# Expert gates in float32: one matmul per token in place of three, with the tokens innermost in the eviction

## The chip, the cores and the metric

The kernel runs on one core of a Trainium2 chip. The metric is the device time of one execution in microseconds, as the median of several runs. The profile is one execution, recorded by the hardware profiler.

## The reference, cut to what is computed

Two transformer blocks in float32 over 256 tokens of width 1024. The first ends in product-key experts, and only these are touched. Each token has 8 heads, each head picks 16 of 128 x 128 experts by two lists of sub-keys, and the gates are a softmax over the 16 scores:

```python
v1, i1 = lax.top_k(s1, PEER_TOPK)
v2, i2 = lax.top_k(s2, PEER_TOPK)
...
top_s, pos = lax.top_k(cand_s, PEER_TOPK)
idx = jnp.take_along_axis(cand_i, pos, axis=-1)
g = jax.nn.softmax(top_s, axis=-1)
u_sel = jnp.take(u_tab, idx, axis=0)
h = jnp.einsum('bthkd,btd->bthk', u_sel, xb)
a = (jax.nn.gelu(h.astype(jnp.float32)) * g).astype(xb.dtype)
return jnp.einsum('bthk,bthkd->btd', a, jnp.take(v_tab, idx, axis=0))
```

An expert's index is `i1 * 128 + i2`. A token thus has 128 picks (8 heads of 16), each with a pair of indices and a gate.

## The kernel before, in words

Nothing is gathered: the kernel multiplies all tokens with all 16,384 rows of the table u, and sets the unpicked experts to nought by a dense matrix of gates. The table comes in 128 chunks of 128 experts (512 KB each, loaded on the queue of SyncE into `rawt`, five ahead). A chunk is split into two parts of 12 significant bits (`wrt` by ScalarE, line 241; `wlt` by VectorE, line 242), and `mm_stat` (lines 447 to 451) multiplies it with the tokens in 24 matmuls of 256 columns. ScalarE evicts through gelu: the first 56 chunks (`NB`) go into `H`, which holds [128 experts, 56 chunks, 256 tokens], the others through `hs` to DRAM (`hsp`), except the last two pairs, which stay. Then `peer_v` reads the table v against the gated values.

Beside the chunks two generators run on VectorE, stepped by counted microseconds (`STEP`: 1.55 a chunk for `select`, 1.7 for `gates`; a step yields what it is reckoned to take). `select` finds the picks: the two top-16 lists, the candidates, the 16 best and their index pairs, and writes them transposed into `picks`, one column per token: row 0 the first index, row 1 the second, row 2 the gate, rows 3 and 4 what bfloat16 leaves of it. When it ends, `gates` starts, one group of four tokens for each chunk of u, 64 groups in all.

A group is one call of `prep` and one of `put`. `prep` compares the second and the first index of the 128 picks with the numbers 0 to 127, which gives one-hot rows [128 picks, 128, 4 tokens] in bfloat16, with the four tokens innermost, and multiplies the first of these with the three parts of the gate. `put` makes, for each token, three matmuls over the 128 picks into one [128, 128] block of gates; VectorE multiplies the first 56 columns of four tokens into `H` (line 848), and ScalarE copies the other 72 into `G` (line 849). `prep` runs one group ahead of `put`, with two buffers for its tiles.

The order of the instructions on each engine is set by a scheduler with a simulated timeline. Those that are pinned (`pin`) keep their place in the program: the first compare of a group, the gate matmuls, and the first matmul of each chunk in this stage. The others may be moved by the scheduler.

Of the kernel before, what the change touches and what calls it, by code (L numbers as in the profile page):

```python
# [8 lines left out]
F32 = mybir.dt.float32  # L9
# [16 lines left out]
WARM = (2.5, 0.5, 2, 1.5)  # keep_warm at the start, after the first transposes, before a block, in the mixer  # L26
STEP = (1.55, 1.7)  # steps of the selection and of the gates per chunk of peer_u
NB = 56  # expert blocks whose activations stay in SBUF
V_AFTER_R = (0, 0, 0, 0, 2, 2, 2, 2)  # chunks of w_v after each chunk of w_r
# [14 lines left out]
def _consts():  # L44
    """Constants of the shapes alone: [128, n] float32 blocks."""
    f = np.float32
    c = {}
    i = np.arange(128)
    c["ident"] = np.eye(128, dtype=f)
    c["iota"] = np.tile(i.astype(f)[None], (128, 1))  # L50
    half = 32
    freqs = (f(10000.0) ** (-np.arange(half, dtype=f) / f(half))).astype(f)
    ang = (np.arange(256, dtype=f)[:, None] * freqs[None]).astype(f)
    cs = np.stack([np.cos(ang), np.sin(ang)], 1).astype(f)
    c["rope"] = cs.reshape(2, 128, 2, 32).transpose(1, 0, 2, 3).reshape(128, 128)
    log_g = np.log1p(-np.exp2(-5.0 - np.arange(8, dtype=np.float64)))
    diff = (i[None, :] - i[:, None]).astype(np.float64)
    dm = np.zeros((128, 8, 256))
    for h in range(8):
        diag = np.where(diff >= 0, np.exp(log_g[h] * np.maximum(diff, 0)), 0)  # L60
        dm[:, h, :128] = diag
        dm[:, h, 128:256] = np.exp(log_g[h] * (diff + 128))
    c["dmask"] = dm.reshape(128, 8 * 256).astype(f)
    c["sblt"] = (i[:, None] < i[None, :]).astype(f)
    c["nsuf"] = -(i[:, None] >= i[None, :]).astype(f)
    p, q = i[:, None], i[None, :]
    same = (p // 64) == (q // 64)
    lt, le = (p < q) & same, (p <= q) & same
    dec = f(-math.exp(-0.5))
    c["tri"] = np.concatenate([le * dec, lt * dec], 1).astype(f)  # L70
    c["m4"] = np.concatenate([lt, lt, le, le], 1).astype(f)
    c["off"] = (same & (p // 16 > q // 16)).astype(f)
    q32 = np.arange(32)[None, :]
    c["m16"] = ((p // 16 % 2 == q32 // 16) & (p % 16 > q32 % 16)).astype(f)
    c["dl"] = (p % 16 == np.arange(16)[None, :]).astype(f)
    c["b8"] = (p // 16 == np.arange(8)[None, :]).astype(f)
    c["blk"] = same.astype(f)
    c["hs2"] = (i[:, None] // 64 == np.arange(2)[None, :]).astype(f)
    return c
# [29 lines left out]
def layout(inp):  # L109
    """Host side: the inputs in the layouts in which the kernel loads them."""  # L110
# [51 lines left out]
class Kern:  # L162
# [37 lines left out]
    def keep_warm(self, us, acc=False):  # L200
        """Matmuls into a bank that nobody reads, so that a wait doesn't halve TensorE's clock."""
# [18 lines left out]
    def add_mixed(self, names, order):  # L220
        """Chunks of several weights in turns: names[j] for each j of order."""
        at = [0] * len(names)
        for j in order:
            self.plan.append((names[j], self.d[names[j]][at[j]]))
            at[j] += 1
# [32 lines left out]
    def after(self, a, b):  # L258
        """a is issued after b, on the same engine."""
        self.tc.add_manual_dep(a.ins, b.ins.name, mybir.DependencyInfo(  # L260
            mybir.DependencyClass.NoSync, mybir.DependencyReason.DATA), reason="order")
# [12 lines left out]
    def steps(self, gens):  # L274
        """Each generator starts one step after the one before it."""
# [12 lines left out]
    def rsqrt(self, x, n, name="rs_y"):  # L288
        """x ** -0.5 on [128, n]."""
# [4 lines left out]
    def split(self, ps, r, l, scale=None, pin=False):  # L294
        """r + l = ps (times scale per partition), both with 12 significant bits."""
# [11 lines left out]
    def transposed(self, pool, src, nk, name, scale=None, plain=False, then=None, pin=False):  # L307
        """src(h, k): token-major [128, 128] blocks -> parts of the transpose, [128, nk, 256]."""
# [28 lines left out]
    def square(self, h, c0, c1, pin=False):  # L337
        """Sum of squares of some columns of the residual; after the last, the inverse norm."""
# [19 lines left out]
    def norm_T(self, pool, name, gname, g0, npool=None, nkw={}, plain=False, then=None):  # L358
        """rms-normalized residual, transposed, in parts."""
# [12 lines left out]
    def turn(self, k):  # L372
        """Two [128, 128] blocks of columns of the residual, transposed, in PSUM."""
# [9 lines left out]
    def res_T(self, pool, gain, pin=False):  # L383
        """The residual times the gain, transposed, in parts; its consumer scales the tokens by the inverse norm."""
# [12 lines left out]
    def uncap(self, n=1 << 30):  # L397
        """Splits of up to n more chunks of weights, in this place of the program."""
# [4 lines left out]
    def mm_mov(self, name, xr, xl, nk, evac, side=1, tail=0, pin=False, halves=True, marks={}):  # L403
        """One group of 512 columns: evac(h, psum) for the token halves h of x @ w.
        The first half is done earlier by the last `tail` chunks of weights."""
        nc = self.nc
        # token half, columns, psum
# [33 lines left out]
    def mm_stat(self, name, xr, xl, out, nk=8, pin=False):  # L441
        """out [128 features, 256 tokens] of the next chunk of weights."""
# [11 lines left out]
    def attn(self):  # L454
        nc, tc, d = self.nc, self.tc, self.d
        with ExitStack() as cx:
# [42 lines left out]
            def qk_norm(accs, idx, scale):  # L499
                """Heads of 64, rms-normalized: [128, 2, 512] token-major, gain not yet applied."""  # L500
# [120 lines left out]
            def pin(a):  # L621
                """Keeps the functions that need tables in their order, so that the tables change seldom."""
# [107 lines left out]
    def peer(self):  # L730
        nc, tc, d = self.nc, self.tc, self.d
        with ExitStack() as cx:
# [3 lines left out]
            with ExitStack() as cu:  # L736
                pu = cu.enter_context(tc.tile_pool(name="pu", bufs=1, reuse_waits="tile"))
                hw = cu.enter_context(tc.tile_pool(name="hw", bufs=2, reuse_waits="tile"))
                picks = pu.tile([128, 5, 256], BF, name="picks")
                H = pu.tile([128, NB, 256], F32, name="H")  # L740
                iota4 = pu.tile([128, 128, 4], BF, name="iota4")
                nc.vector.tensor_copy(iota4, self.iota[:, :, None].to_broadcast([128, 128, 4]))
# [25 lines left out]
                def select():  # L768
                    """Yields about the microseconds of VectorE that each step takes."""
# [5 lines left out]
                    for t in range(2):  # L775
# [44 lines left out]
                        nc.scalar.copy(picks[:, 0:3, tt], pt)  # L820
                        low = tk.tile([128, 128], F32, name="low")
                        nc.vector.tensor_tensor(low, pt[:, 2], picks[:, 2, tt], op=OP.subtract)
                        nc.scalar.copy(picks[:, 3, tt], low)
                        nc.vector.tensor_tensor(picks[:, 4, tt], low, picks[:, 3, tt], op=OP.subtract)
                        yield 1.3

                def gates(G):
                    """Per token: one-hot rows of the picks times the gates in three exact parts."""
                    def prep(t0):
                        ts = slice(t0, t0 + 4)  # L830
                        pk = [picks[:, None, j, ts].to_broadcast([128, 128, 4]) for j in range(5)]
                        oa = hw.tile([128, 2, 128, 4], BF, name="oa", tag="ar")
                        ob = hw.tile([128, 2, 128, 4], BF, name="ob", tag="al")
                        o = [oa[:, 0], oa[:, 1], ob[:, 0], ob[:, 1], oa[:, 0]]
                        pin(nc.vector.tensor_tensor(o[0], iota4, pk[0], op=OP.is_equal))
                        nc.vector.tensor_tensor(o[1], iota4, pk[1], op=OP.is_equal)
                        for j in range(2, 5):
                            nc.vector.tensor_tensor(o[j], o[0], pk[j], op=OP.mult)
                        return t0, o

                    def put(t0, o):
                        pg = self.sm.tile([128, 4, 128], F32, name="smt")
                        for t in range(4):
                            for j in range(2, 5):
                                pin(nc.tensor.matmul(pg[:, t], o[1][:, :, t], o[j][:, :, t],  # L845
                                                     start=(j == 2), stop=(j == 4)))
                        hv = H[:, :, t0:t0 + 4].rearrange("p i t -> p t i")
                        nc.vector.tensor_tensor(hv, pg[:, :, :NB], hv, op=OP.mult)  # L848
                        nc.scalar.copy(G[:, :, t0:t0 + 4].rearrange("p i t -> p t i"), pg[:, :, NB:])

                    old = prep(0)
                    yield 3
                    for t0 in range(4, 260, 4):
                        new = prep(t0) if t0 < 256 else None
                        put(*old)
                        old = new
                        yield 1.7
# [97 lines left out]
    def top16(self, pool, jobs, n):  # L955
        """The 16 largest of each x [128, n], largest first, and where they first stand: (val, idx, x)."""
# [121 lines left out]
    def rwkv(self):  # L1078
        nc, tc, d = self.nc, self.tc, self.d
        with ExitStack() as cx:  # L1080
# [36 lines left out]
            with ExitStack() as c1:  # L1117
# [17 lines left out]
                def chain(pt, k):  # L1135
                    """Parts of the mix for K, straight from the transposes, before what the others need."""
# [106 lines left out]
            with ExitStack() as c2:  # L1243
# [23 lines left out]
                def values():  # L1267
                    """Steps of one chunk of weights: 256 features of x @ w_v, token-major."""
# [16 lines left out]
                def prep(i, wk, M32):  # L1285
                    """Decayed A, B, K, R of two heads, in the places of their sources; M = A B^T."""
# [42 lines left out]
                def subst(i0, i1, wk, M32, sel):  # L1329
                    """Transposed inverses of the unit lower triangular 16 x 16 blocks, a row at a time."""  # L1330
# [302 lines left out]
```

## Time and profile before

| what | value |
|---|---|
| median of 3 runs | 1861.52 us (1861.39 to 1861.53) |
| span of the profiled execution, first to last instruction | 1859.7 us |
| PE (TensorE matmul) busy | 1844.6 us, 99% |
| DVE (VectorE) busy | 1348.8 us, 73% |
| ACT (ScalarE) busy | 990.7 us, 53% |
| gate matmuls, line 845 | 768 records, 483.7 to 755.8 us |

The profile gives no time for its execution other than the span; the runs' median is 1.8 us longer. The busy time of an engine is the union of its instructions. Matmuls are pipelined, so a record is longer than the time for which it holds the engine; the distance from one start to the next tells what it costs. PEld are the weight loads of TensorE, which run beside its matmuls.

### The profile page before, as it was taken

To read this page: it belongs to the slowest core of one execution; us is meant where nothing else is said; L and a number is where in the kernel's file an instruction comes from. 1 tells how busy PE (TensorE), PEld (TensorE's weight loads), DVE (VectorE), ACT (ScalarE), POOL (GpSimd) and SP (SyncE) were. 2 spreads that over 40 slices of the span, in tenths; PEclk is the share of its full clock that TensorE was granted. 3 is DMA by queue.
4 is the path that set the end of the run, shared out by engine and by line. 5 is a ranking of instruction groups with operands and counts; after the bars stand their busy time and mean duration, and the time that the engine had idled before them with its cause. 6 is when DMAs were issued, how large, how long until landed. Compare 5 with 4: busy or idle time off the path is not lost.

```text
span 1859.7 us, 31176 instructions
## 1 busy us (share of the span) xinstructions
PE 1844.6 (99%) x12249; PEld 1662.3 (89%) x12249; DVE 1348.8 (73%) x2532; ACT 990.7 (53%) x1557; POOL 63.6 (3%) x60
## 2 busy tenths in 40 slices
PE   9999999999999999999999999999999999999998
PEld 7877899999999999888888888899887988879997
DVE  6755668899888888655666667688657886558874
ACT  6468554445544444544444455566456744456653
POOL 1110000000000000000000000000002011000000
PEclk9999999999999999999999999999999999999999
DMA  7454545555644445556777755555653320035553
GB/s 276 138 169 147 173 149 169 182 182 181 187 150 158 154 154 156 186 192 196 221 269 240 242 193 181 158 184 182 229 173 97 117 67 1 1 103 190 185 186 121
DMA packets 90450, 308.59 MB, mean 166 GB/s; under 512 B 9981, under 2 KB 11517, under 8 KB 89918
## 3 DMA queue, kind: packets, MB, share of 16 engines
q1 hardware_dynamic: 90014, 306.07, 50.8%
q8 instruction: 96, 1.57, 0.3%
q10 hardware_dynamic: 288, 0.52, 0.1%
q14 instruction: 52, 0.43, 0.1%
HBM read 296.59 MB, written 9.96 MB: 165 GB/s over the span
## 4 chain that ended last, share of the span: by engine, by line
PE 97%; DVE 2%; DMA 1%; ACT 0%; issue 0%; SPq 0%; POOL 0%; POOLq 0%; ACTq 0%
PE acct L451 13%; PE acct L447 13%; PE acct L450 13%; PE acct L420 7%; PE acct L421 7%; PE acct L415 6%; PE acct L929 6%; PE acct L933 6%; PE acct L932 6%; PE smt L845 5%; PE acct L1423 1%; PE acct L1209 1%; PE smt L1394 1%; DVE wlt L242 0%; PE acct L1278 0%; PE acct L1279 0%
## 5 line engine op out<-in xcount | busy, mean ns | idle before, releaser
L242 DVE TENSOR_TENSOR wlt<-rawt,wrt 128x1024 fp32r<-128x1024 f32 x532 | 650.9, 1225 | 280.3 <-ACT wrt L241 278.9
L241 ACT CAST wrt<-rawt 128x1024 fp32r<-128x1024 f32 x532 | 556.1, 1046 | 296.8 <-PE acct L421 106.6
L447 PE MATMUL acct<-XR,wrt 128*128 128x256 f32 x1920 | 549.0, 287 | 0.0
L451 PE MATMUL acct<-XL,wrt 128*128 128x256 f32 x1920 | 542.7, 283 | 1.0 <-DVE XL L302 1.0
L450 PE MATMUL acct<-XR,wlt 128*128 128x256 f32 x1920 | 543.5, 283 | 0.0
L447 PEld LDWEIGHTS acct<-XR,wrt 128*128 128x128 f32 x1920 | 368.3, 192 | 1.6 <-issue 0.9
L451 PEld LDWEIGHTS acct<-XL,wrt 128*128 128x128 f32 x1920 | 367.3, 192 | 2.2 <-DVE XL L302 2.2
L450 PEld LDWEIGHTS acct<-XR,wlt 128*128 128x128 f32 x1920 | 368.0, 192 | 0.5 <-issue 0.2
L932 PE MATMUL acct<-wlt,ar 128*128 128x512 f32 x512 | 182.1, 389 | 0.0
L933 PE MATMUL acct<-wrt,al 128*128 128x512 f32 x512 | 181.6, 389 | 0.0
L929 PE MATMUL acct<-wrt,ar 128*128 128x512 f32 x512 | 138.9, 389 | 0.0
L420 PE MATMUL acct<-wlt,XR 128*128 128x512 f32 (+1 forms) x304 | 118.5, 391 | 0.5 <-DVE wlt L242 0.5
L421 PE MATMUL acct<-wrt,XL 128*128 128x512 f32 (+1 forms) x304 | 116.7, 392 | 0.0
L933 PEld LDWEIGHTS acct<-wrt,al 128*128 128x128 f32 x512 | 96.1, 188 | 20.0
L932 PEld LDWEIGHTS acct<-wlt,ar 128*128 128x128 f32 x512 | 96.1, 188 | 19.9
L929 PEld LDWEIGHTS acct<-wrt,ar 128*128 128x128 f32 x512 | 96.1, 188 | 19.9
L415 PE MATMUL acct<-wrt,XR 128*128 128x512 f32 (+1 forms) x304 | 112.1, 394 | 0.5 <-ACT wrt L241 0.5
L1069 ACT ACTIVATE z<-acct,cols 128x256 f32<-128x256 f32 x88 | 49.8, 566 | 90.9 <-PE acct L451 90.9
L845 PE MATMUL smt<-ob,oa 128*128 128x128 bf16 x512 | 93.9, 296 | 0.0
L845 PEld LDWEIGHTS <-oa 128*128 128x128 bf16 x768 | 81.7, 118 | 3.8
L877 ACT ACTIVATE hs<-acct 128x256 f32<-128x256 f32 x72 | 27.9, 387 | 105.7 <-PE acct L451 105.7
L848 DVE TENSOR_TENSOR H<-smt,H 128x224 f32<-128x224 f32 x64 | 42.9, 670 | 46.1 <-PE smt L845 46.1
(422 smaller groups left out, 2827.4 us busy)
## 6 DMA issues: line engine op xcount, KB each, us to landing
rawt<-in_peer_u SPq DMA_DIRECT2D x128, 512.0 KB, 3.5
rawt<-in_peer_v SPq DMA_DIRECT2D x128, 512.0 KB, 3.5
rawt<-in_ffn_up SPq DMA_DIRECT2D x88, 512.0 KB, 3.5
rawt<-in_w_in SPq DMA_DIRECT2D x52, 512.0 KB, 4.2
rawt<-in_ffn_dn SPq DMA_DIRECT2D x44, 512.0 KB, 3.4
hsp<-hs SPq DMA_DIRECT2D x34, 256.0 KB, 3.9
hs<-hsp SPq DMA_DIRECT2D x34, 256.0 KB, 3.6
rawt<-in_peer_wq SPq DMA_DIRECT2D x16, 512.0 KB, 3.6
```

The costliest lines, as they stand in the source:

```text
L241: c = nc.scalar.copy(r, t)
L242: v = nc.vector.tensor_tensor(l, t, r.bitcast(F32), op=OP.subtract)
L415: m = nc.tensor.matmul(o, a, wr, start=(k == 0), stop=False)
L420: nc.tensor.matmul(o, a, wl, start=False, stop=False)
L421: nc.tensor.matmul(o, b, wr, start=False, stop=(k == nk - 1))
L447: m = nc.tensor.matmul(out, wr, xr[:, k], start=(k == 0), stop=False)
L450: nc.tensor.matmul(out, wl, xr[:, k], start=False, stop=False)
L451: nc.tensor.matmul(out, wr, xl[:, k], start=False, stop=(k == nk - 1))
L845: pin(nc.tensor.matmul(pg[:, t], o[1][:, :, t], o[j][:, :, t], start=(j == 2), stop=(j == 4)))
L929: m = nc.tensor.matmul(acc[t][c], a, wr, start=first, stop=False)
L932: nc.tensor.matmul(acc[t][c], a, wl, start=False, stop=False)
L933: nc.tensor.matmul(acc[t][c], b, wr, start=False, stop=last)
```

## The change

The picks are kept in float32 (three rows instead of five), and the copy of the numbers 0 to 127, repeated for four tokens, goes. `prep` makes two float32 tiles [128 picks, 4 tokens, 128], with the 128 numbers innermost: the one-hot rows of the second index, and those of the first index times the gate. That is two compares and one product where two compares and three products were. `put` makes one float32 matmul per token. The eviction reads the block of gates with the tokens innermost, so `H` and `G` are touched in runs of four tokens, and PSUM with a stride of 128 elements. Comments go, and a constant `TG` of 4 comes; the groups and their steps stay.

```diff
+TG = 4
...
-                picks = pu.tile([128, 5, 256], BF, name="picks")
+                picks = pu.tile([128, 3, 256], F32, name="picks")
                 H = pu.tile([128, NB, 256], F32, name="H")
-                iota4 = pu.tile([128, 128, 4], BF, name="iota4")
-                nc.vector.tensor_copy(iota4, self.iota[:, :, None].to_broadcast([128, 128, 4]))
...
-                        nc.scalar.copy(picks[:, 0:3, tt], pt)
-                        low = tk.tile([128, 128], F32, name="low")
-                        nc.vector.tensor_tensor(low, pt[:, 2], picks[:, 2, tt], op=OP.subtract)
-                        nc.scalar.copy(picks[:, 3, tt], low)
-                        nc.vector.tensor_tensor(picks[:, 4, tt], low, picks[:, 3, tt], op=OP.subtract)
-                        yield 1.3
+                        nc.scalar.copy(picks[:, :, tt], pt)
+                        yield 0.8
...
                     def prep(t0):
-                        ts = slice(t0, t0 + 4)
-                        pk = [picks[:, None, j, ts].to_broadcast([128, 128, 4]) for j in range(5)]
-                        oa = hw.tile([128, 2, 128, 4], BF, name="oa", tag="ar")
-                        ob = hw.tile([128, 2, 128, 4], BF, name="ob", tag="al")
-                        o = [oa[:, 0], oa[:, 1], ob[:, 0], ob[:, 1], oa[:, 0]]
-                        pin(nc.vector.tensor_tensor(o[0], iota4, pk[0], op=OP.is_equal))
-                        nc.vector.tensor_tensor(o[1], iota4, pk[1], op=OP.is_equal)
-                        for j in range(2, 5):
-                            nc.vector.tensor_tensor(o[j], o[0], pk[j], op=OP.mult)
-                        return t0, o
+                        ts = slice(t0, t0 + TG)
+                        io = self.iota[:, None, :].to_broadcast([128, TG, 128])
+                        pk = [picks[:, j, ts][:, :, None].to_broadcast([128, TG, 128]) for j in range(3)]
+                        o1 = hw.tile([128, TG, 128], F32, name="oa", tag="ar")
+                        o2 = hw.tile([128, TG, 128], F32, name="ob", tag="al")
+                        pin(nc.vector.tensor_tensor(o1, io, pk[1], op=OP.is_equal))
+                        nc.vector.tensor_tensor(o2, io, pk[0], op=OP.is_equal)
+                        nc.vector.tensor_tensor(o2, o2, pk[2], op=OP.mult)
+                        return o1, o2
...
-                            for j in range(2, 5):
-                                pin(nc.tensor.matmul(pg[:, t], o[1][:, :, t], o[j][:, :, t],
-                                                     start=(j == 2), stop=(j == 4)))
-                        hv = H[:, :, t0:t0 + 4].rearrange("p i t -> p t i")
-                        nc.vector.tensor_tensor(hv, pg[:, :, :NB], hv, op=OP.mult)
-                        nc.scalar.copy(G[:, :, t0:t0 + 4].rearrange("p i t -> p t i"), pg[:, :, NB:])
+                            pin(nc.tensor.matmul(pg[:, t], o1[:, q + t], o2[:, q + t], start=True, stop=True))
+                        pg = pg.rearrange("p t i -> p i t")
+                        hv = H[:, :, t0:t0 + 4]
+                        nc.vector.tensor_tensor(hv, pg[:, :NB], hv, op=OP.mult)
+                        nc.scalar.copy(G[:, :, t0:t0 + 4], pg[:, NB:])
...
-                    for t0 in range(4, 260, 4):
-                        new = prep(t0) if t0 < 256 else None
-                        put(*old)
+                    for t0 in range(0, 256, TG):
+                        new = prep(t0 + TG) if t0 + TG < 256 else None
+                        for q in range(0, TG, 4):
+                            put(t0 + q, *old, q)
+                            yield 1.7
                         old = new
-                        yield 1.7
```

## Rows read from the trace of the kernel before

**Rows 1.** The page: busy time of each engine, and the chain that ended last.

```profile
PE 1844.6 (99%) x12249; PEld 1662.3 (89%) x12249; DVE 1348.8 (73%) x2532; ACT 990.7 (53%) x1557; POOL 63.6 (3%) x60
...
PE 97%; DVE 2%; DMA 1%; ACT 0%; issue 0%; SPq 0%; POOL 0%; POOLq 0%; ACTq 0%
```

**Rows 2.** Windows, selection and gate stage: length, busy us, clock, DMA, GB/s.

```profile
310.00:470.00 160.00, 160.00 (x1336) 160.00 (x1335) 145.38 (x330) 76.69 (x117) 0.00 (x0) 1.00 0.57 181
480.00:757.00 277.00, 277.00 (x2324) 273.05 (x2323) 228.07 (x449) 130.59 (x197) 0.00 (x0) 1.00 0.50 156
```

**Rows 3.** The chain that ended last, gate stage: start us, us, what.

```profile
599.98 1.43 PE smt L845 x12
...
655.84 1.42 PE smt L845 x12
```

**Rows 4.** Timeline, PE in the gate stage: start us, us, engine, line, operation.

```profile
599.82 0.41 PE L845 MATMUL smt<-ob,oa 128*128 128x128 bf16 x2
...
601.16 0.37 PE L447 MATMUL acct<-XR,wrt 128*128 128x256 f32 x1
...
601.36 0.29 PE L450 MATMUL acct<-XR,wlt 128*128 128x256 f32 x1
...
604.12 0.41 PE L845 MATMUL smt<-ob,oa 128*128 128x128 bf16 x2
```

**Rows 5.** Timeline, PE around the matmuls of the scores, line 762.

```profile
256.29 0.28 PE L450 MATMUL acct<-XR,wlt 128*128 128x256 f32 x1
256.41 0.61 PE L762 MATMUL smt<-kT,pq 128*128 128x128 f32 x4
256.77 0.36 PE L451 MATMUL acct<-XL,wrt 128*128 128x256 f32 x1
256.98 0.28 PE L447 MATMUL acct<-XR,wrt 128*128 128x256 f32 x1
```

**Rows 6.** Timeline, PE in the second block, line 1415 and after.

```profile
1512.26 1.06 PE L1415 MATMUL acct<-RH,T 128*128 128x128 f32 x8
1513.07 0.36 PE L1347 MATMUL smt<-mr,sel 128*128 128x256 f32 x1
1513.28 0.28 PE L1348 MATMUL smt<-ml,sel 128*128 128x256 f32 x1
```

**Rows 7.** Groups of DVE in the gates: count, busy us, mean ns, idle before.

```profile
L838 DVE TENSOR_TENSOR ob<-oa,picks 128x512 bf16<-128x512 bf16 x128 | 48.6, 421 | 2.1
L848 DVE TENSOR_TENSOR H<-smt,H 128x224 f32<-128x224 f32 x64 | 42.9, 670 | 46.1 <-PE smt L845 46.1
```

**Rows 8.** Groups of DVE elsewhere, float32 with a broadcast or PSUM operand.

```profile
L799 DVE TENSOR_TENSOR eq<-abf,cs 128x2048 f32<-128x2048 f32 x4 | 9.1, 2286 | 0.0
...
L1397 DVE TENSOR_TENSOR WB<-smt,crw 128x512 f32<-128x512 f32 x8 | 5.5, 684 | 0.2
...
L1355 DVE TENSOR_TENSOR M<-smt,TT 128x224 f32<-128x224 f32 x2 | 0.8, 392 | 0.1
```

**Rows 9.** Timeline, DVE over one period of the gate stage.

```profile
601.44 0.67 DVE L848 TENSOR_TENSOR H<-smt,H 128x224 f32<-128x224 f32 x1 [0.71 <-PE smt L845]
...
602.03 0.42 DVE L836 TENSOR_TENSOR oa<-iota,picks 128x512 bf16<-128x512 bf16 x1
...
602.36 0.42 DVE L838 TENSOR_TENSOR oa<-oa,picks 128x512 bf16<-128x512 bf16 x1
...
602.70 1.22 DVE L242 TENSOR_TENSOR wlt<-rawt,wrt 128x1024 fp32r<-128x1024 f32 x1
```

**Rows 10.** Timeline, DVE at the entry of the experts.

```profile
244.72 0.16 DVE L348 SCALAR_TENSOR_TENSOR ssq<-ssq 128x1 f32<-128x1 f32 x1 [0.30 <-ACT sqs L342]
```

**Rows 11.** Groups of PEld, the weight loads of TensorE.

```profile
L845 PEld LDWEIGHTS <-oa 128*128 128x128 bf16 x768 | 81.7, 118 | 3.8
...
L762 PEld LDWEIGHTS smt<-kT,pq 128*128 128x128 f32 x64 | 8.6, 192 | 0.0
```

**Rows 12.** Timeline, the weight loads of line 762.

```profile
256.29 0.54 PEld L762 LDWEIGHTS smt<-kT,pq 128*128 128x128 f32 x4
```

More of the change, by code (lines that the diff above doesn't have):

```diff
@@ L836, in prep @@
-                        nc.vector.tensor_tensor(o[1], iota4, pk[1], op=OP.is_equal)
-                        for j in range(2, 5):
-                            nc.vector.tensor_tensor(o[j], o[0], pk[j], op=OP.mult)
-                        return t0, o
-                    def put(t0, o):
+                        ts = slice(t0, t0 + TG)
+                        io = self.iota[:, None, :].to_broadcast([128, TG, 128])
+                        pk = [picks[:, j, ts][:, :, None].to_broadcast([128, TG, 128]) for j in range(3)]
@@ L842, in put @@
+                        o1 = hw.tile([128, TG, 128], F32, name="oa", tag="ar")
[4 more added lines that the diff above has]
+                        return o1, o2
+                    def put(t0, o1, o2, q):
                         pg = self.sm.tile([128, 4, 128], F32, name="smt")
```

## The prediction

> **What bounds the kernel now.** I read the page's first parts [rows 1]: TensorE (PE) is busy in 99% of the span, and the chain that ended last is 97% PE. So a microsecond of PE work taken out is a microsecond off the time, until another engine is late. A busy PE is not yet a PE at its rate, so the next view is the stage that the change touches. [...]
>
> Then the cadence. In the gate stage each chunk of peer_u, 24 matmuls, is followed by one group of four tokens. The chain shows the groups at 599.98 and, 13 groups later, at 655.84 us [rows 3], 4.297 us apiece. The chunk's matmuls follow each other after 0.12 us (256.29 to 256.41 [rows 5]), so a chunk is 24 × 0.12 = 2.88 us, and a group costs PE 4.297 − 2.88 = 1.417 us. The timeline of PE [rows 4] agrees: the twelve bfloat16 matmuls start at 599.82 and the next chunk at 601.16 us, 1.34 us, and that chunk's second matmul comes 0.20 us behind its first instead of 0.12, another 0.08. The 64 groups are 64 × 1.417 = 90.7 us of the span.
>
> **The change part by part.** *Matmuls.* Twelve per group go, four float32 ones come. What a float32 matmul of 128x128 by 128 columns costs is in the trace, because the scores multiply plain float32 tiles (line 762): the code has 32 of these matmuls and the trace 64 weight loads [rows 11], and a run of two matmuls shows four records [rows 5], so one matmul is two loads and two records. The four records start at 256.41, the next line's matmul at 256.77 and its second at 256.98 us; taking off 0.12 for that matmul, two float32 matmuls cost 0.45 us, switch included. A run as long as ours stands at line 1415, four matmuls in eight records: 1512.26 to 1513.07 us, then 0.21 to the second matmul of the next line [rows 6]: 0.81 + 0.09 = 0.90 us, which is twice 0.45. I take 0.90. The low bound is that run without any switch, 0.81; the high bound is eight records paced like the loads of line 762, (0.54 − 0.19)/3 = 0.117 us apart [rows 11, 12], plus 0.09: 1.03. The saving is 1.417 − 0.90 = 0.517 us a group, 33.1 us for 64; the bounds give 64 × 0.607 = 38.8 and 64 × 0.387 = 24.8 us. The new operands are packed, as those of lines 762 and 1415 are, so I add nothing for the access.
>
> *One-hots.* DVE's five bfloat16 operations a group, about 0.42 us each [rows 7], become three in float32 of the same 512 elements. Float32 operations with a broadcast operand are in the trace at 2048 elements, 2.29 us for a compare (line 799), and at 512, 0.68 us for a product (line 1397) [rows 8]. That is 2.05 us for 2.10: nothing won. It would not show anyway, as DVE waits 0.71 us in a period for the group's matmuls ahead of the product [rows 9].
>
> *Eviction.* The product with H takes 0.670 us for 224 elements [rows 7]; one that reads PSUM in contiguous runs and has the same count takes 0.392 [rows 8]. The excess, 0.28, is what single elements 1 KB apart in H cost. With tokens innermost H and G are touched in runs of four, but PSUM is read with a hop of 512 bytes at every element, and no row shows a PSUM read like that. Bounds: 0.39 (the hop is free) to 0.95 (it costs the 0.28 once more over today's 0.67). I take 0.67, what a single hopping side costs now. ScalarE's copy into G changes likewise, but that engine is busy only 130.59 of 277 us [rows 2].
>
> [...]
>
> *Is DVE still under PE?* The new period would be 2.88 + 0.90 = 3.78 us. DVE's records overlap by 0.09 us (0.42 long at 602.03, the next at 602.36 [rows 9]). Its work is three one-hot operations (0.60, 0.60, and 0.69 for one that needs the other), the weight split 1.22 − 0.09 = 1.13, the product 0.67 − 0.09 = 0.58: 3.60 us, 0.18 below the period; 3.32 with the cheap eviction, 3.88 with the dear one, which is 0.10 above.
>
> *The rest.* The float32 picks drop one ScalarE and two DVE operations per half, and the widened iota goes, a DVE operation of 512 elements, 0.42 us by the price above. It stands between two residual operations at the entry of the stage, but DVE waits 0.30 us for ScalarE right after it [rows 10], so most of it hides: 0.1 us at most, which I leave out. The counted steps make the selection 1.0 us shorter by its own yields; run through by hand they start the groups one chunk earlier and leave all 64 ahead of the last chunk, as now. No DMA is moved; with the shorter period the loads and the spill have to go at 156 × 4.297/3.78 = 177 GB/s, where the selection stage ran at 181 without a PE gap [rows 2].
>
> **The sum.** 64 × 0.517 = 33.1 us off a span of 1859.7. The runs' median, 1861.52, is 1.8 us over that span, and I leave those 1.8 as they are: 1861.5 − 33.0 = 1828.5 us.
>
> **The rivals.** *A, PE-bound all the way (75%):* 1823 to 1837 us by the bounds, 1828.5 the likeliest.
>
> *B, DVE becomes the bound (7%).* If the PSUM hop is dear, the period is 3.88 and 64 × 0.10 = 6 us are given back: 1835 us. For it: no row excludes the hop's price. Against it: the cheap bound is as near to the rows as the dear one.
>
> *C, the order on VectorE gives part back (11%).* The product waits for the group's matmuls, and all that stands behind it on DVE waits too. Counted from the first matmul of the next chunk, the product starts 0.28 us later (601.16 to 601.44 [rows 4, 9]) and the next group's first matmul is due after 2.96 us (604.12 [rows 4]). Before, two of the five one-hot operations stood behind the product, and the split behind them [rows 9]. Now the unpinned compare and product of the one-hots can stand there: 0.28 + 0.58 + 0.60 + 0.69 = 2.15, in time. With the split ahead of them it is 3.28, and PE waits 0.32 us a group, 20 us: 1849.
>
> *D, slower (4%).* The same place, but with all three one-hot operations and the split behind the product: 0.28 + 0.58 + 1.13 + 0.60 + 0.60 + 0.69 = 3.88 us, 0.92 late, so 64 × (0.92 − 0.517) = 26 us are lost: 1888. It turns into a loss from 0.517 us of lateness on. Against it: before, the last one-hot operation ended at 602.78 for a group that began at 604.12 us [rows 4, 9], 1.34 us early, and the first compare is pinned ahead of the product.
>
> *E, the weight loads set the pace (3%).* A float32 load takes 192 ns where the bfloat16 one takes 118 [rows 11]. Eight in a row without overlap would be 1.54 us for 1.417: 8 us lost, 1869. Against it: the four loads of line 762 take 0.54 us together [rows 12], so they overlap, and these starts are in my 0.45. [...]
>
> **How the numbers follow.** The range runs from A's low bound, 1823, to 1840, some way beyond A's high bound and B, to take in a small C; the rest of C, and D and E, lie above, some 15 in 100 together with what A may miss. A measurement of this kernel can tell about 0.2%, 3.7 us, from no change. A, B and C are faster by more (93%), a C that eats nearly all is the same (2%), D and E are slower (5%, after rounding).
>
> **What would show it.** In the profile of the changed kernel: 512 float32 records in place of line 845's 768, in steps of about 0.11 us; groups 3.78 us apart; PE busy throughout the stage; DVE's idle time before the product down from 46.1 us [rows 7] to about 64 × 0.18 = 12; the product at 0.4 to 0.7 us. The prediction is wrong if the period is well over 3.8: with PE waiting for a one-hot that is C or D; with a DVE that never idles, B; with records 0.19 us apart, E.

## The result, and the profile after

The changed kernel takes 1833.76 us (median of 4 runs, 1833.27 to 1834.60) where the kernel before took 1861.53 in the same comparison: the ratio is 0.9851, 95% interval 0.9839 to 0.9863. The gain is 27.8 us; the forecast was 33.0. The profiled span is 1831.6 us, 28.1 below that of before.

The page shows the same picture as [rows 1]: PE busy in 99% of a shorter span, and the chain nearly all PE.

```profile
PE 1812.9 (99%) x11993; PEld 1634.1 (89%) x11993; DVE 1333.2 (73%) x2399; ACT 971.7 (53%) x1555; POOL 64.9 (4%) x60
...
PE 96%; DVE 2%; ACT 0%; issue 0%; DMA 0%; POOL 0%; SPq 0%; POOLq 0%; DVEq 0%; ACTq 0%
```

The chain in the gate stage answers to [rows 3]. The groups stand at 600.11 and, 15 groups later, at 656.61 us, 3.767 us apiece, so a group costs PE 3.767 − 2.88 = 0.887 us where it cost 1.417.

```profile
600.11 0.89 PE smt L838 x8
...
656.61 0.89 PE smt L838 x8
```

The timeline of PE answers to [rows 4]: eight records start at 599.95, the next chunk at 600.76, its second matmul 0.20 us later. Those are the 0.81 us and, within a hundredth, the pause of 0.21 of line 1415 [rows 6].

```profile
599.95 1.06 PE L838 MATMUL smt<-ob,oa 128*128 128x128 f32 x8
600.76 0.36 PE L448 MATMUL acct<-XR,wrt 128*128 128x256 f32 x1
600.96 0.28 PE L451 MATMUL acct<-XR,wlt 128*128 128x256 f32 x1
...
603.71 1.06 PE L838 MATMUL smt<-ob,oa 128*128 128x128 f32 x8
```

The groups of DVE answer to [rows 7]: three one-hot operations of 0.68 us, and the product with H (line 841) at 0.391 us, down from 0.670. Its wait for PE is 29.9 us in all.

```profile
L830 DVE TENSOR_TENSOR oa<-cs,picks 128x512 f32<-128x512 f32 x64 | 43.8, 685 | 0.0
L832 DVE TENSOR_TENSOR ob<-ob,picks 128x512 f32<-128x512 f32 x64 | 43.7, 684 | 0.0
L831 DVE TENSOR_TENSOR ob<-cs,picks 128x512 f32<-128x512 f32 x64 | 43.5, 681 | 0.0
...
L841 DVE TENSOR_TENSOR H<-smt,H 128x224 f32<-128x224 f32 x64 | 25.0, 391 | 29.9 <-PE smt L838 29.9
```

By the groups alone, 64 × (1.417 − 0.887) = 33.9 us should have gone, but the span fell by 28.1, so 5.8 came back. The windows show where (length; busy us of PE, PEld, DVE, ACT, POOL; clock; DMA; GB/s). Between 474 and 480 us PE is busy for only 2.15 of 6 us, and the granted clock, 1.00 before, is 0.91, then 0.50 and 0.74 before it is 1.00 again.

```profile
474.00:478.00 4.00, 1.71 (x13) 1.31 (x11) 4.00 (x4) 2.57 (x3) 0.00 (x0) 1.00 0.76 231
478.00:480.00 2.00, 0.44 (x3) 0.47 (x4) 1.93 (x5) 0.36 (x3) 0.00 (x0) 0.91 0.69 229
480.00:482.00 2.00, 2.00 (x11) 2.00 (x11) 0.01 (x1) 1.74 (x2) 0.00 (x0) 0.50 0.58 225
482.00:484.00 2.00, 2.00 (x15) 2.00 (x15) 0.00 (x0) 0.00 (x0) 0.00 (x0) 0.74 0.00 0
484.00:486.00 2.00, 2.00 (x19) 2.00 (x19) 0.38 (x1) 1.32 (x2) 0.00 (x0) 1.00 0.00 0
```

The timeline of PE names the instruction: two of the three transposes (line 817) of the second half of the picks, each waiting for an operation of DVE, 1.99 and 1.86 us, 3.85 together. After them the chunk's matmuls come 0.21 us apart instead of 0.12: 15 of them take 3.34 us from 479.61 to 482.95, 1.54 more than at full clock.

```profile
475.10 0.28 PE L452 MATMUL acct<-XL,wrt 128*128 128x256 f32 x1
477.37 0.33 PE L817 MATMUL smt<-cs,sel 128*128 128x128 f32 x1 [1.99 <-DVE sel L806]
479.56 0.39 PE L817 MATMUL smt<-cs,sel 128*128 128x128 f32 x1 [1.86 <-DVE sel L814]
479.61 0.55 PE L448 MATMUL acct<-XR,wrt 128*128 128x256 f32 x1
...
482.95 0.33 PE L448 MATMUL acct<-XR,wrt 128*128 128x256 f32 x1
```

The chain through the same stretch is all VectorE from 475.31 to 479.42 us: the last reduction of the selection, the softmax, and a weight split of 1.14 us between them. The two losses make 5.39 us: 33.9 − 3.85 − 1.54 = 28.5 us, where the spans differ by 28.1. The other 0.4 us are not traced.

```profile
475.31 2.00 DVE sel L806
477.31 0.20 DVE sel L810
477.51 1.14 DVE wlt L243
478.65 0.21 DVE pesum L812
478.88 0.21 DVE pesum L813
479.12 0.30 DVE sel L814
```

In the order of TensorE's instructions the second and third transpose stand together, straight ahead of the first matmul of a chunk, and all that follows waits with them (a row of this listing is one instruction or a run of equal ones):

```
2899 L452 MATMUL acct_5037<-XL_2191,wrt_4971 128x256
2900 L817 MATMUL smt_5076<-cs_77,sel_4768 128x128 x2
2901 L448 MATMUL acct_5092<-XR_2190,wrt_5005 128x256
```

In the kernel before they stood 97 and 169 rows behind the first transpose of that half, the last one after a group of gates; now both stand 71 rows behind it. The place in the program thus explains the wait, and the experiments ask what moved the two.

### The profile page after: what moved, and what is told of

Same layout as the page of the kernel before. It is cut to its first block, busy times and chain, and to the rows that moved or that the text cites. A ratio compares the mean times of both kernels' runs of the same rounds, so it can differ in the third digit from the quotient of the medians.

```text
span 1831.6 us, 30595 instructions
## 1 busy us (share of the span) xinstructions
PE 1812.9 (99%) x11993; PEld 1634.1 (89%) x11993; DVE 1333.2 (73%) x2399; ACT 971.7 (53%) x1555; POOL 64.9 (4%) x60
## 3 DMA queue, kind: packets, MB, share of 16 engines
q8 instruction: 94, 1.54, 0.3%
## 4 chain that ended last, share of the span: by engine, by line
PE 96%; DVE 2%; ACT 0%; issue 0%; DMA 0%; POOL 0%; SPq 0%; POOLq 0%; DVEq 0%; ACTq 0%
PE acct L452 13%; PE acct L448 13%; PE acct L451 13%; PE acct L421 7%; PE acct L422 7%; PE acct L416 7%; PE acct L926 6%; PE acct L927 6%; PE acct L923 6%; PE smt L838 3%; PE acct L1417 1%; PE acct L1203 1%; PE smt L1388 1%; DVE wlt L243 0%; PE acct L1272 0%; PE acct L1273 0%
## 5 line engine op out<-in xcount | busy, mean ns | idle before, releaser
L421 PEld LDWEIGHTS acct<-wlt,XR 128*128 128x128 f32 x304 | 57.1, 188 | 13.1 <-DVE wlt L243 1.0
L1064 DVE SCALAR_TENSOR_TENSOR z<-acct,cols,z 128x255 f32<-128x255 f32 x88 | 42.5, 483 | 35.5 <-ACT z L1063 35.4
L416 PEld LDWEIGHTS acct<-wrt,XR 128*128 128x128 f32 x304 | 56.5, 188 | 12.8 <-ACT wrt L242 1.1
```

The lines of the kernel that those rows point to most:

```text
L416: m = nc.tensor.matmul(o, a, wr, start=(k == 0), stop=False)
L421: nc.tensor.matmul(o, a, wl, start=False, stop=False)
```

## The experiments

### What moved the transposes

One line of the change is only a number: the last step of the selection yields 0.8 instead of 1.3. Run through by hand, the old number lets the budget of chunk 59 end with that step, and the first group is prepared, and the pins start, one chunk later; with the new one all of it falls to chunk 59. Put back in the changed kernel:

```diff
                         nc.scalar.copy(picks[:, :, tt], pt)
-                        yield 0.8
+                        yield 1.3
```

> The changed kernel with one number put back: the last step of the selection is again reckoned at 1.3 us instead of 0.8, so that the groups start one chunk later, as they did before; no computation is touched. Theory 1 (the 5 us that the forecast lacks are a wait of PE for the transposes of the second half of the picks, 475.1 to 479.6 us, plus the clock at 0.50 to 0.91 after it, and the wait comes from where the scheduler puts those transposes once the groups start a chunk earlier): the wait and the clock dip go, PE is busy from 470 to 490 us, and the time falls by 3.85 us of idle and about 1.5 us of slow matmuls to 1828.4 us. Theory 2 (the wait belongs to the float32 picks or to the shorter chain behind them, whatever the steps): the wait stays and the time is 1833.8 us.

Measured: 1827.6 us, ratio to before 0.9817 (0.9804 to 0.9830). The transposes are parted again in the order (49 and 93 rows after the place where they stood together), and the windows show PE busy throughout at a clock of 1.00:

```profile
474.00:478.00 4.00, 4.00 (x36) 4.00 (x35) 4.00 (x4) 1.32 (x2) 0.00 (x0) 1.00 0.69 232
478.00:480.00 2.00, 2.00 (x19) 2.00 (x18) 1.59 (x3) 1.92 (x3) 0.00 (x0) 1.00 0.67 231
480.00:482.00 2.00, 2.00 (x19) 2.00 (x18) 1.14 (x3) 1.97 (x3) 0.00 (x0) 1.00 0.50 203
```

Its span is 33.8 us below that of before, and the groups account for 33.9. The reverse, the number alone in the kernel before:

```diff
                         nc.vector.tensor_tensor(picks[:, 4, tt], low, picks[:, 3, tt], op=OP.subtract)
-                        yield 1.3
+                        yield 0.8
```

> The kernel before with only that number changed, 1.3 to 0.8 us; the three bfloat16 matmuls and the old eviction stay. Theory 1: the kernel before gets the wait of PE near 475 us and the clock dip, and takes about 5 us longer, 1867 us. Theory 2: no wait, 1861.5 us.

Measured: 1867.2 us, ratio 1.0030 (1.0018 to 1.0043), 5.5 us longer than before. The timeline of PE shows the same wait there, without any float32 gate:

```profile
475.19 0.27 PE L818 MATMUL smt<-cs,sel 128*128 128x128 f32 x1
479.35 0.45 PE L818 MATMUL smt<-cs,sel 128*128 128x128 f32 x1 [3.90 <-DVE sel L815]
```

So theory 1 holds in both directions: the 5 to 6 us belong to the reckoned step and to the order that the scheduler makes of it, not to the float32 picks. Why its simulated timeline puts the two transposes there was not looked into and stays open.

### The eviction

In the changed kernel, the old order:

```diff
-                        pg = pg.rearrange("p t i -> p i t")
-                        hv = H[:, :, t0:t0 + 4]
-                        nc.vector.tensor_tensor(hv, pg[:, :NB], hv, op=OP.mult)
-                        nc.scalar.copy(G[:, :, t0:t0 + 4], pg[:, NB:])
+                        hv = H[:, :, t0:t0 + 4].rearrange("p i t -> p t i")
+                        nc.vector.tensor_tensor(hv, pg[:, :, :NB], hv, op=OP.mult)
+                        nc.scalar.copy(G[:, :, t0:t0 + 4].rearrange("p i t -> p t i"), pg[:, :, NB:])
```

> The changed kernel with the old eviction (columns innermost, H and G touched 1 KB apart), everything else as changed. Theory of the prediction (the eviction hides behind PE): the product is back at 0.67 us from 0.39, VectorE's work rises from 3.33 to 3.61 us a period and stays under the 3.77 of PE, its wait before the product falls from 0.44 to about 0.16 us, and the time stays at 1833.8 us. Rival (the eviction is part of the gain): the period is longer than 3.77 us, 64 x 0.28 = 18 us at most, 1852 us.

Measured: 1833.8 us, ratio to before 0.9849 (0.9834 to 0.9864), the same as the changed kernel. The product is back at 0.677 us and its wait is down to 8.4 us for 61, 0.14 apiece:

```profile
L840 DVE TENSOR_TENSOR H<-smt,H 128x224 f32<-128x224 f32 x61 | 41.3, 677 | 9.5 <-PE smt L838 8.4
```

The kernel before with the new eviction (the same lines the other way):

> The kernel before with only the new eviction (tokens innermost). Theory of the prediction: the product falls from 0.67 to about 0.39 us and ScalarE's copy from 0.69 to 0.40, and the time stays at 1861.5 us, since VectorE then only waits longer. Rival (part of the gain is the eviction's): several us faster, down to 1843 us if all 0.28 us a group were on the path.

Measured: 1861.8 us, ratio 1.0000 (0.9991 to 1.0009). The product takes 0.391 us, 0.28 less, and the wait ahead of it grows from 0.72 us apiece (46.1 for 64 [rows 7]) to 0.97, so most of the saving is spent waiting:

```profile
L849 DVE TENSOR_TENSOR H<-smt,H 128x224 f32<-128x224 f32 x54 | 21.1, 391 | 52.5 <-PE smt L845 52.5
```

The eviction is worth nothing in time in either kernel; it gives VectorE room.

### The price of a float32 matmul, and of VectorE's work

In this part the base is the version with the step put back, 1827.6 us. It was measured in another comparison than the runs here, but the kernel before took 1861.67 us there and 1861.66 here.

```diff
                             pin(nc.tensor.matmul(pg[:, t], o1[:, q + t], o2[:, q + t], start=True, stop=True))
+                            pin(nc.tensor.matmul(pg[:, t], o1[:, q + t], o2[:, q + t], start=True, stop=True))
```

> The version with the step put back to 1.3 us (1827.6 us), and each gate matmul issued twice into the same place, so the result is the same. Theory of the prediction (PE sets the pace of the gate stage, and four float32 matmuls cost 0.81 us beside 0.08 for the switch): 64 x 0.81 = 52 us more, 1879 us, and the added records 0.11 us apart. Rival (a good part of a group's time is a wait or the switch, not the matmuls, or a second matmul with the same weights is cheaper): clearly less than 40 us more.

Measured: 1884.7 us, ratio to before 1.0123 (1.0106 to 1.0140). That is 57.1 us more, 0.892 us a group and 0.1115 a record. The expectation was 5 us short because it took 0.81 for the matmuls and 0.08 for a switch. No switch shows: eight more records cost 0.892 us, as much as a whole group (0.887), so the 0.08 that the next chunk's second matmul comes late belongs to the matmuls too.

```diff
                         pin(nc.vector.tensor_tensor(o1, io, pk[1], op=OP.is_equal))
+                        pin(nc.vector.tensor_tensor(o1, io, pk[1], op=OP.is_equal))
```

> The version with the step put back to 1.3 us, and the first compare of each group made twice on VectorE, with the same result. VectorE's work goes from 3.33 to 3.93 us a period of 3.77. Theory 1 (VectorE's slack is the 0.44 us that it waits before the product, and beyond it every microsecond counts): 64 x 0.16 = 10 us more, 1838 us, with no wait left before the product. Theory 2 (rivals C and D: what stands behind the product is already late, so the order decides and not the sum): all of 64 x 0.60 = 38 us, 1866 us. Theory 3 (VectorE is two groups ahead and never matters): 1827.6 us.

Measured: 1838.1 us, ratio to before 0.9874 (0.9857 to 0.9890): 10.5 us more, theory 1. VectorE's slack is the wait ahead of the product, and here it is used up, 2.3 us for 51. The loss comes in bursts: from 500 to 700 us PE waits 9 times for the added compare (line 831), 7.2 us in all, while other groups start on time:

```profile
L842 DVE TENSOR_TENSOR H<-smt,H 128x224 f32<-128x224 f32 x51 | 19.6, 384 | 2.6 <-PE smt L839 2.3
```

### Float32, or packed rows?

The change does two things to the matmuls at once: one float32 for three bfloat16, and operands whose 128 columns lie side by side instead of four elements apart. In the kernel before, packed rows alone (with the new eviction):

```diff
-                iota4 = pu.tile([128, 128, 4], BF, name="iota4")
-                nc.vector.tensor_copy(iota4, self.iota[:, :, None].to_broadcast([128, 128, 4]))
+                iota4 = pu.tile([128, 4, 128], BF, name="iota4")
+                nc.vector.tensor_copy(iota4, self.iota[:, None, :].to_broadcast([128, 4, 128]))
...
-                        pk = [picks[:, None, j, ts].to_broadcast([128, 128, 4]) for j in range(5)]
-                        oa = hw.tile([128, 2, 128, 4], BF, name="oa", tag="ar")
-                        ob = hw.tile([128, 2, 128, 4], BF, name="ob", tag="al")
+                        pk = [picks[:, j, ts][:, :, None].to_broadcast([128, 4, 128]) for j in range(5)]
+                        oa = hw.tile([128, 2, 4, 128], BF, name="oa", tag="ar")
+                        ob = hw.tile([128, 2, 4, 128], BF, name="ob", tag="al")
...
-                                pin(nc.tensor.matmul(pg[:, t], o[1][:, :, t], o[j][:, :, t],
+                                pin(nc.tensor.matmul(pg[:, t], o[1][:, t], o[j][:, t],
```

> The kernel before, three bfloat16 matmuls per token, but with packed rows (the 128 numbers innermost, the tokens outside) and the new eviction. It parts the two halves of the change: one float32 matmul for three, and packed rows for rows 8 bytes apart. Theory 1 (the rows 8 bytes apart cost the time: 128 such columns took 0.112 us, as long as 256 packed float32r columns): the records come about 0.06 us apart, twelve take some 0.72 us, less than the 0.81 of four float32 ones. Theory 2 (a weight load and a matmul of this size take 0.11 us whatever the layout): twelve take 1.34 us as before. The time is then VectorE's or PE's: if the five one-hot operations take 0.68 us instead of 0.42, as the broadcast operand now stands still along the innermost dimension, its work is about 4.45 us a period and the time near 1871 us; if they stay at 0.42, 1822 us by theory 1 and 1861 us by theory 2.

Measured: 1872.1 us, ratio 1.0057 (1.0040 to 1.0074), slower than before. The timeline of PE shows the matmuls as theory 1 has them, ten starts from 624.64 to 625.14 us, 0.056 apart, so twelve would cost 0.67 us; but the first of these ten waited 0.67 us for a one-hot:

```profile
624.64 0.22 PE L845 MATMUL smt<-oa 128*128 128x128 bf16 x1 [0.67 <-DVE oa L838]
624.69 0.27 PE L845 MATMUL smt<-ob,oa 128*128 128x128 bf16 x2
...
625.14 0.22 PE L845 MATMUL smt<-oa 128*128 128x128 bf16 x1
625.17 0.36 PE L447 MATMUL acct<-XR,wrt 128*128 128x256 f32 x1
```

The one-hot operations are at 0.68 us, in bfloat16 as in float32, and VectorE never waits in its window:

```profile
L836 DVE TENSOR_TENSOR oa<-iota,picks 128x512 bf16<-128x512 bf16 x45 | 30.7, 682 | 0.0
L835 DVE TENSOR_TENSOR oa<-iota,picks 128x512 bf16<-128x512 bf16 x45 | 30.6, 679 | 0.0
L849 DVE TENSOR_TENSOR H<-smt,H 128x224 f32<-128x224 f32 x45 | 17.2, 381 | 0.0
```

The other half, float32 with the tokens innermost, again against the version with the step put back:

```diff
-                        io = self.iota[:, None, :].to_broadcast([128, TG, 128])
-                        pk = [picks[:, j, ts][:, :, None].to_broadcast([128, TG, 128]) for j in range(3)]
-                        o1 = hw.tile([128, TG, 128], F32, name="oa", tag="ar")
-                        o2 = hw.tile([128, TG, 128], F32, name="ob", tag="al")
+                        io = self.iota[:, :, None].to_broadcast([128, 128, TG])
+                        pk = [picks[:, None, j, ts].to_broadcast([128, 128, TG]) for j in range(3)]
+                        o1 = hw.tile([128, 128, TG], F32, name="oa", tag="ar")
+                        o2 = hw.tile([128, 128, TG], F32, name="ob", tag="al")
...
-                            pin(nc.tensor.matmul(pg[:, t], o1[:, q + t], o2[:, q + t], start=True, stop=True))
+                            pin(nc.tensor.matmul(pg[:, t], o1[:, :, q + t], o2[:, :, q + t], start=True, stop=True))
```

> The version with the step put back to 1.3 us, one float32 matmul per token, but the tokens innermost in the one-hot tiles as before, so that the matmul reads and loads columns 16 bytes apart. Theory 1 (rows that are not packed cost PE): the records are further apart than 0.11 us, up to 0.21 if it is the same factor as in bfloat16, 64 x 0.8 = 51 us more, 1879 us. Theory 2 (the layout is without effect on float32): 1827.6 us.

Measured: 1897.1 us, ratio 1.0190 (1.0173 to 1.0207), 69.5 us over the base. The chunk starts 1.78 us after the first of the eight records, and its second matmul comes after another 0.30, so a group costs 1.78 + 0.30 − 0.12 = 1.96 us. The first record holds PE for 0.30 us, the next six for 0.235 each; packed ones come 0.1115 apart.

```profile
619.98 2.13 PE L838 MATMUL smt<-ob,oa 128*128 128x128 f32 x8
621.76 0.46 PE L448 MATMUL acct<-XR,wrt 128*128 128x256 f32 x1
622.06 0.28 PE L451 MATMUL acct<-XR,wlt 128*128 128x256 f32 x1
```

The chain of this run says the same, where it had 1.43 us for twelve records before [rows 3] and 0.89 for eight in the changed kernel:

```profile
620.14 1.96 PE smt L838 x8
```

So the matmuls alone tell the halves apart. Twelve bfloat16 ones cost 1.42 us strided, 0.118 apiece, and 0.67 packed; eight float32 records cost 1.96 and 0.89. In these runs the weights and the moving columns change their layout together, so which of the two makes a strided matmul dear is not shown. Float32 is the dearer of the two on PE in either layout; the gain on PE is the packing, and float32 is what makes the packed one-hots few enough for VectorE.

### Packed bfloat16 with cheaper one-hots

If twelve packed bfloat16 matmuls cost 0.22 us less than the float32 ones, 14 us would be left to win if VectorE kept up. Two versions made the products per token, with the picks kept in float32 (the second version makes the compare of the second index per token too; the lines below show the products alone):

```diff
-                        for j in range(2, 5):
-                            nc.vector.tensor_tensor(o[j], o[0], pk[j], op=OP.mult)
+                        for t in range(4):
+                            p = lambda j: picks[:, j, t0 + t:t0 + t + 1]
+                            for j in range(2, 5):
+                                nc.vector.tensor_scalar(o[j][:, t], iota4, p(0), p(j), op0=OP.is_equal, op1=OP.mult)
```

> The packed bfloat16 version (1872.1 us), whose twelve matmuls take 0.67 us but whose five one-hot operations of 0.68 us bind VectorE, with the three products made otherwise: for each token one operation of 128 elements compares the numbers with the first index and multiplies with one part of the gate, both taken per partition; the second index keeps its compare of 512 elements. Twelve short operations and one long take the place of five long ones. Theory 1 (a short 16-bit operation holds VectorE for about 0.15 us): 0.60 + 1.80 + 1.13 + 0.31 = 3.84 us a period against 3.63 for PE, so 2.88 + 0.96, 1832 us. Theory 2 (the fixed part of an operation rules, 0.2 us and more each): 4.44 us or longer, 1871 us and more. If the short ones take 0.13 us or less, PE binds at 3.63: 1819 us.

> The same with the compare of the second index also made in four short operations, sixteen short ones in all. If a short one holds VectorE for 0.15 us, this and the one before are alike (3.84 us a period, 1832 us); if less, this one is the faster, down to PE's 3.63 us and 1819 us; if more, the slower by 64 times four of the differences.

Measured: 1884.8 us (ratio 1.0127, 1.0110 to 1.0144) and 1887.6 us (1.0140, 1.0123 to 1.0157). The first came out by theory 2, and the second does not differ from it beyond the intervals. A compare with a product of 128 elements holds VectorE for about 0.22 us (three from 620.11 to 620.78 in the first of the two), so twelve take 2.7 us where 1.8 were hoped for:

```profile
620.11 0.54 DVE L841 TENSOR_SCALAR ob<-iota,picks 128x128 bf16<-128x128 bf16 x2
...
620.78 0.54 DVE L841 TENSOR_SCALAR ob<-iota,picks 128x128 bf16<-128x128 bf16 x2
```

In the second, where all sixteen are short, VectorE is busy all the time as well:

```profile
L841 DVE TENSOR_SCALAR ob<-iota,picks 128x128 bf16<-128x128 bf16 x336 | 87.9, 300 | 0.0
...
L837 DVE TENSOR_SCALAR oa<-iota,picks 128x128 bf16<-128x128 bf16 x169 | 40.5, 240 | 0.0
L852 DVE TENSOR_TENSOR H<-smt,H 128x224 f32<-128x224 f32 x42 | 15.8, 375 | 0.0
```

No version beat the changed kernel with the step put back, 1827.6 us.

## Why the prediction was right, point by point

**The bound and the matmuls: right.** PE set the pace of the stage, and the group came out at 0.887 us for the 0.90 taken from lines 762 and 1415. The measured 33.9 us of the groups stand beside 33.1 in the sum (of which it took off 33.0). The 0.08 or 0.09 of "switch" in the working is no cost of its own, as the doubled matmuls show; the total was right. "I add nothing for the access" was right for packed operands, but the prediction passed over how much hangs on it: in the old layout the same float32 matmuls cost 1.96 us a group (the groups of that version start at 619.98 and 624.82 us, 4.84 apart), more than the 1.417 of before, and the change would have been a loss.

**"The rest": the step that failed.** The prediction saw that the selection is reckoned 1.0 us shorter and the groups start a chunk earlier, and booked it at nothing, because all 64 still end before the last chunk. It looked at the far end of the shift only. At the near end the shift changed the order in which the scheduler placed the last transposes, and PE waited 3.85 us for VectorE and ran slowly for some 3.3 more: 5 to 6 us, shown from both sides by the first two experiments. With the old step the time is 1827.6, 6.2 us less, so this is more than the whole difference of 5.3 us between 1828.5 and 1833.8; the groups, 0.8 us cheaper than the sum had them, make up most of the rest. That 1833.8 still lies between A's bounds is luck: those bounds were for the price of a matmul, and nothing in the range was meant for this loss.

**The one-hots: right.** 0.68 us each, as from lines 799 and 1397.

**The eviction: the bound was right, the value taken was not.** The product took the low bound, 0.39 us (0.391), and not the 0.67 of the sum: a PSUM read that hops 512 bytes at every element takes what the contiguous one took, 0.392 [rows 8]. That put VectorE's wait at 0.44 us a group instead of 0.18 (28 us in all and not 12), with no effect on the time, as the two runs on the eviction show. Rival B is out for this kernel; the old eviction in the changed kernel shows how near it was, with 0.14 us of slack at 0.677 us, against the 0.18 of the working.

**Rivals C and D: the arrangement came, the delay did not.** What D feared stands in the trace. The timeline of DVE has a compare, the split, a compare and a product behind the product with H:

```profile
601.04 0.39 DVE L841 TENSOR_TENSOR H<-smt,H 128x224 f32<-128x224 f32 x1 [0.44 <-PE smt L838]
601.35 0.68 DVE L831 TENSOR_TENSOR ob<-cs,picks 128x512 f32<-128x512 f32 x1
601.95 1.22 DVE L243 TENSOR_TENSOR wlt<-rawt,wrt 128x1024 fp32r<-128x1024 f32 x1
603.08 0.69 DVE L830 TENSOR_TENSOR oa<-cs,picks 128x512 f32<-128x512 f32 x1
603.68 0.68 DVE L832 TENSOR_TENSOR ob<-ob,picks 128x512 f32<-128x512 f32 x1
604.81 0.39 DVE L841 TENSOR_TENSOR H<-smt,H 128x224 f32<-128x224 f32 x1 [0.44 <-PE smt L838]
```

But these one-hots are not for the group that starts at 603.71. In the program they come ahead of that group's own product with H (604.81), so they are for the next one, at 607.48 us, and end 3.1 us early. C and D counted to the wrong group, one period too soon; `prep` running one group ahead is exactly what gives that period. So what counts here is the sum of VectorE's work, which the added compare measured: 0.60 us more a group cost 10.5 us in all, 0.16 a group, which is what lies beyond the slack.

**Rival E: out.** The loads take 192 ns each and the records come 0.11 us apart, so the loads overlap.

## What to carry to other kernels

Before pricing a matmul by its type, look at the distance between its columns: here a stride of four elements somewhat more than doubled the cost of a matmul in both types (0.118 us for 0.056 in bfloat16, 0.49 for 0.223 in float32), and packing gained more than either choice of type (0.75 and 1.07 us a group, against 0.22 packed and 0.54 strided). Where a generator is stepped by reckoned microseconds, a change of those numbers is a change of the order of the program, and the place to look is both ends of the shift: a stall of 4 us beside a gain of 34 is easily taken for noise in the gain. When counting what is late behind a wait, first find which iteration the waiting work belongs to; a stage that is prepared one ahead has a whole period more than it seems.

## What the runs showed of the hardware

- A float32 matmul of 128 columns with packed operands cost 0.223 us (two records of 0.1115); strided by 16 bytes it cost 0.49, a quarter of the 1.96 us of a group. A bfloat16 one cost 0.056 us packed and 0.118 strided by 8 bytes. The weight loads of the strided float32 operands took 329 ns on average, those of the packed ones 192; in bfloat16 they took 118 strided and 97 packed. The loads and the moving columns were never strided apart from each other.
- Reads of PSUM by VectorE and ScalarE with a hop of 512 bytes at every element cost nothing that shows: 0.391 us for VectorE's 224 elements, where runs of 14 took 0.392 (line 1355 of the kernel before), and 0.400 us for ScalarE's 288, where 256 contiguous ones took 0.384 in its gelu (line 871). The hops that cost were the single elements 1 KB apart in SBUF, 0.670 and 0.69 us for the same two operations before.
- Two waits of 1.99 and 1.86 us, with one transpose between them, were followed by a granted clock of 0.50, and the 256-column matmuls came 0.21 us apart instead of 0.12; with PE busy again from 479.56 us on, the clock was back at 1.00 in the window from 484 us.
